# The head of a conditioned decoder layer: column groups of the modulation by output block, five slices, and an instruction order written out

## The chip, the core and the metric

The kernel runs on one core of one Trainium2 chip. A core has five engines that run side by side, each through its own instructions in order: TensorE (PE, matrix products out of SBUF into PSUM), VectorE (DVE), ScalarE (ACT), GpSimd (POOL) and SyncE (SP). SP and POOL also issue the transfers between HBM and SBUF, each on a queue of its own, and 16 DMA engines carry them. The metric is the device time of one execution in microseconds; lower is better.

## The reference, cut to what matters

One layer runs on 256 prompt rows and 8 x 8 sample rows (320 columns in the kernel, where everything is held transposed). Each of the nine sequences (one prompt, eight samples) has a conditioning vector `c`.

```python
mod = silu(c) @ w_ada + b_ada                 # w_ada: 2048 x (6*2048)
sh1, sc1, g1, sh2, sc2, g2 = split(mod, 6)
h = rmsnorm(x, norm1_g) * (1 + sc1) + sh1
p = h @ w_in                                  # q k v og u ga gb and a narrow gate input
o, s_new = gla(q, k, v, loga, s0)             # gated linear attention, 4 heads
merged = sigmoid(ga) * (rmsnorm(o) * silu(og)) + sigmoid(gb) * pool(u)
x = x + g1 * (merged @ w_o)
h2 = rmsnorm(x, norm2_g) * (1 + sc2) + sh2
x = x + g2 * ((silu(gate) * up) @ w_down)     # gate, up = split(h2 @ w_gu)
```

Outputs are the normed x of both groups, the attention states and the pooling buffers. The head, the part that the change is about, is everything up to `h` and the first quarter of `h @ w_in`: the columns of attention head 0, called group 0.

## The kernel before

**Tiles.** The 2048 input features are 16 blocks of 128 (`KT`). `hh[k]` and `hl[k]` are the high and the low part of block k of h, 128 x 320. A weight arrives as fp32 in a `raw` tile; `split` (line 146) makes its high part on ACT (line 151) and its low part on DVE (line 152), 512 columns at a time; `mm3` (line 164) then makes three products, lines 165 to 167. Group 0 has eleven units of 256 output columns (q, k, two of v, u, two each of og, ga, gb).

**Why there are slices.** The section products of w_ada for shift (section 0) and scale (section 1) must be there before a block of h can be made, and w_ada is large: 2 x 16.8 MB for these two sections. So the head runs over slices of the 16 blocks, `SLICES` (line 39): blocks 0-1, 2-3, 4-7 and 8-15. For each slice all units of group 0 are multiplied with the blocks of that slice and added up in SBUF (`evac`, line 349: the first slice writes, on ACT or DVE; the later ones add on DVE, lines 356, 358 and 369). Meanwhile the next slice's blocks are made in the background: the list `bg` (line 493) holds `hada` for section 0, `hada` for section 1, and `h_unit`, for two blocks at a time, and is worked off evenly between the units.

**One `ada` call** (line 214) makes one section for two blocks: four loads of 512 KB on SP's queue into a ring of seven buffers, 16 matmuls with 256 columns of w_ada as moving data, four of them side by side in 32-column strips of the array, each strip summing every fourth input block; then a copy to SBUF (line 228), two transposes, a reduction over the four strips (line 233), and the additions of bias, one and norm weight (lines 236 to 240).

**One `h_unit`** (line 454) takes per block three transposes of the x rows, a copy to `xT` on ACT, which POOL stores to DRAM for later (line 463), the scaling by the row norm (line 462), `affine` (lines 320 to 322) and `hilo` (lines 315 and 316).

**Units.** q, k and u go through `proj` (256 columns, one PSUM tile of the two in pool `pmain`); v, og, ga and gb through `proj2` (line 196: 512 columns, both PSUM tiles at once).

**What sets the order.** A scheduler that simulates the program's timeline picks each engine's order out of the source, with source order as priority; it may pull later work forward. All w_in and w_ada loads of the head are on SP's queue, in an order that it chose. Eight loads of a queue may be under way; a ninth waits for the first. In the second half of the head the narrow gate projection `alr_proj` (line 467) runs, and group 0's first attention steps begin before the last units end.

Behind the head stand the other three heads' projections with attention steps of the head before between them, the sections 4, 2, 3 and 5 of w_ada in bursts (`ada_burst`, line 273), then w_o, w_gu and w_down. None of that is edited.

Of the kernel before, what the change touches and what calls it, by code (L numbers as in the profile page):

```python
# [11 lines left out]
F32 = mybir.dt.float32  # L12
# [8 lines left out]
P = 128  # L21
TP, NB, LS = 256, 8, 8
TS = NB * LS
T = TP + TS
# [14 lines left out]
SLICES = ((0, 2), (2, 4), (4, 8), (8, 16))  # L39
# [43 lines left out]
def body(tc, A):  # L83
# [112 lines left out]
    def proj2(w, col, k0, k1, xh, xl):  # L196

        pp = [pmain.tile([P, 2, 512], F32, tag="pm", name=nm("ps")) for _ in range(2)]
        for c0 in range(k0, k1, 2):
            nk = min(2, k1 - c0)  # L200
            for j, whi, wlo in split_chunk(w[:, c0:c0 + nk, col:col + 512], nk, 512):
                kt = c0 + j
                for i in range(4):
                    mm3(pp[i // 2][:, i % 2, :T], whi[:, i * P:(i + 1) * P], wlo[:, i * P:(i + 1) * P],
                        xh[kt], xl[kt], kt == k0, kt == k1 - 1)
        return pp

# [5 lines left out]

    def ada(sec, b0, nb=2, pool=None, bufs=2):

        pool = pool or apool[0]
        blk = sec * KT + b0
        w = nb * P
        ps = misc()
        step = 8 // nb  # L220
        for k0 in range(0, KT, step):
            raw = raw_chunk(wada[:, k0:k0 + step, blk * P:(blk + nb) * P], step, w, pool, "araw", bufs)
            for i in range(step):
                j, r = (k0 + i) % 4, (k0 + i) // 4
                PE.matmul(ps[32 * j:32 * j + 32, 0:w], lhsT=scT[:, k0 + i, :], rhs=raw[:, i, :],
                          start=r == 0, stop=r == 3, tile_position=(0, 32 * j))
        sb = pool.tile([P, w], F32, tag="adasb", name=nm("adasb"))
        S.copy(sb, ps[:, 0:w])
        pt = misc()
        for i in range(nb):  # L230
            tr(pt[:, i * P:(i + 1) * P], sb[:, i * P:(i + 1) * P])
        dst = mod[:, blk:blk + nb, :]
        V.tensor_reduce(dst, pt[:, 0:w].rearrange("p (b j r) -> p b r j", b=nb, j=4)[:, :, 0:9, :],
                        axis=AX.X, op=ALU.add)
        bb = bada[:, blk:blk + nb].unsqueeze(2).broadcast_to([P, nb, 9])
        V.tensor_tensor(dst, dst, bb, op=ALU.add)
        if sec in (1, 4):
            g = N1G if sec == 1 else N2G
            V.tensor_scalar(dst, dst, 1.0, None, op0=ALU.add)
            V.tensor_tensor(dst, dst, g[:, b0:b0 + nb].unsqueeze(2).broadcast_to([P, nb, 9]), op=ALU.mult)  # L240


# [69 lines left out]
    hl = [hp.tile([P, T], F32R, tag="hl%d" % k, name="hl%d" % k) for k in range(KT)]  # L312
# [5 lines left out]
    def affine(x, a, b, kt):  # L318

        V.tensor_scalar(x[:, 0:TP], x[:, 0:TP], modp(a, kt), modp(b, kt), op0=ALU.mult, op1=ALU.add)  # L320
        V.tensor_tensor(s3(x[:, TP:T]), s3(x[:, TP:T]), mods(a, kt), op=ALU.mult)
        V.tensor_tensor(s3(x[:, TP:T]), s3(x[:, TP:T]), mods(b, kt), op=ALU.add)
# [74 lines left out]
    with tc.tile_pool(name="head", bufs=1) as xp:  # L397
        junk = xp.tile([P, D], F32, name="junk")
        crow = junk[0:9, :]
        nc.sync.dma_start(crow[0:1, :], A["c_prompt"])  # L400
        nc.sync.dma_start(crow[1:9, :], A["c_sample"])
        xn = [xp.tile([P, D], F32, name="xn%d" % i) for i in range(3)]
        G.memset(xn[2][TS:P], 0.0)
        x2d = A["x_prompt"][0]
        V.memset(scT, 0.0)
        make_identity(nc, ident)
        pt = misc()
        for k in range(KT):
            tr(pt[:, 16 * k:16 * k + 9], crow[:, k * P:(k + 1) * P])
# [15 lines left out]
        def hada(sec, b, nb):  # L425
            ada(sec, b, nb, *head_ring)
# [692 lines left out]
```

## Time and profile before

| | us |
|---|---|
| median of 3 runs | 1977.53 (1976.45 to 1977.74) |
| the profiled execution | 1978.01 |
| its span, first to last instruction | 1976.2 |
| first product of group 0 starts | 40.62 |
| last product of the head ends | 254.3 |
| PE busy in the span | 1927.1 |

The profile is of one execution. Per engine it gives the busy time; the windows give the same for stretches of the span, with the clock granted to PE, the mean busy share of the 16 DMA engines and their GB/s. In a group of instructions stand line, engine, operation, the tiles (out<-in), the count, then busy time and mean duration, then the idle time before them and what ended it. PEld is PE's loading of stationary weights. SPq and POOLq are the queues that issue transfers. A fp32 matmul appears as two records, one with the high and low parts (fp32r) as one.

### The profile page before, as it was taken

How to read it: one execution, taken by the hardware profiler on the slowest of the kernel's cores; microseconds unless marked ns; L12 is line 12 of the kernel's file. 1: busy time of each engine (PE TensorE's matmuls, PEld its weight loads, DVE VectorE, ACT ScalarE, POOL GpSimd, SP SyncE). 2: the span in 40 equal slices, each digit the busy share in tenths (PEclk: the TensorE clock that was granted, in tenths of full speed). 3: DMA queues.
4: the chain of work that ended last, by engine and by line, in shares of the span. 5: the costliest groups of instructions: out<-in, count | busy, mean ns of one | idle time of the engine just before them, and what ended most of it. 6: DMA issues, size and time to landing. Idle time of an engine off the chain costs nothing.

```text
span 1976.2 us, 34764 instructions
## 1 busy us (share of the span) xinstructions
PE 1927.1 (98%) x13852; PEld 1812.4 (92%) x13852; DVE 1005.3 (51%) x1905; ACT 822.5 (42%) x1469; POOL 184.7 (9%) x332
## 2 busy tenths in 40 slices
PE   5999999999999999999999999999999999999997
PEld 3778998988899889988989999999999999999997
DVE  2655655656356535665474444444444444444554
ACT  3323553643336433553354333433333434344443
POOL 1002201221121102111130000000000000000000
PEclk9999999999999999999999999999999999999998
DMA  9995558758865787478944554444444444444442
GB/s 323 342 337 184 198 171 282 254 185 307 281 225 165 270 294 260 129 260 319 326 150 159 183 189 142 150 150 144 158 145 151 150 150 150 151 150 148 149 139 97
DMA packets 310044, 400.93 MB, mean 203 GB/s; under 512 B 12865, under 2 KB 273825, under 8 KB 309545
## 3 DMA queue, kind: packets, MB, share of 16 engines
q1 hardware_dynamic: 279754, 291.17, 45.7%
q0 software_dynamic: 30128, 107.55, 14.7%
q8 instruction: 108, 1.77, 0.4%
q14 instruction: 54, 0.44, 0.1%
HBM read 374.23 MB, written 24.67 MB: 202 GB/s over the span
## 4 chain that ended last, share of the span: by engine, by line
PE 82%; DMA 2%; ACT 1%; DVE 1%; issue 0%; POOL 0%; ACTq 0%; DVEq 0%; POOLq 0%
PE ps L167 25%; PE ps L165 25%; PE ps L166 25%; PE pm L284 3%; PE pm L129 1%; DMA araw<-w_ada 1%; PE pm L779 1%; PE pm L758 1%; PE pm L723 1%; DMA raw<-w_o 1%; DMA raw<-w_in 1%; PE pm L712 0%; DVE wlo L152 0%; PE pm L653 0%; ACT whi L151 0%
## 5 line engine op out<-in xcount | busy, mean ns | idle before, releaser
L152 DVE TENSOR_TENSOR wlo<-raw,whi 128x512 fp32r<-128x512 f32 x952 | 655.7, 693 | 784.3 <-ACT whi L151 773.0
L151 ACT CAST whi<-raw 128x512 fp32r<-128x512 f32 x952 | 586.1, 621 | 919.4 <-PE ps L166 830.2
L165 PE MATMUL ps<-hh,whi 128*128 128x320 f32 x1408 | 442.5, 315 | 2.8 <-ACT whi L151 2.1
L167 PE MATMUL ps<-hh,wlo 128*128 128x320 f32 x1408 | 436.8, 313 | 2.0 <-DVE wlo L152 1.9
L166 PE MATMUL ps<-hl,whi 128*128 128x320 f32 x1408 | 437.0, 311 | 0.0
L165 PE MATMUL ps<-h2h,whi 128*128 128x320 f32 x1408 | 434.6, 309 | 0.0
L166 PE MATMUL ps<-h2l,whi 128*128 128x320 f32 x1408 | 434.3, 309 | 0.0
L167 PE MATMUL ps<-h2h,wlo 128*128 128x320 f32 x1408 | 434.2, 309 | 0.0
L165 PEld LDWEIGHTS ps<-hh,whi 128*128 128x128 f32 x1408 | 265.1, 188 | 27.2 <-issue 16.2
L167 PEld LDWEIGHTS ps<-hh,wlo 128*128 128x128 f32 x1408 | 264.2, 188 | 17.6 <-issue 9.1
L166 PEld LDWEIGHTS ps<-hl,whi 128*128 128x128 f32 x1408 | 265.3, 188 | 4.2 <-issue 3.2
L165 PEld LDWEIGHTS ps<-h2h,whi 128*128 128x128 f32 x1408 | 264.5, 188 | 1.2 <-ACT ah L315 1.2
L166 PEld LDWEIGHTS ps<-h2l,whi 128*128 128x128 f32 x1408 | 264.5, 188 | 0.0
L167 PEld LDWEIGHTS ps<-h2h,wlo 128*128 128x128 f32 x1408 | 264.4, 188 | 0.0
L165 PE MATMUL ps<-ah,whi 128*128 128x320 f32 x704 | 217.7, 309 | 0.0
L166 PE MATMUL ps<-al,whi 128*128 128x320 f32 x704 | 216.5, 308 | 0.0
L167 PE MATMUL ps<-ah,wlo 128*128 128x320 f32 x704 | 216.5, 308 | 0.0
L166 PEld LDWEIGHTS ps<-al,whi 128*128 128x128 f32 x704 | 132.0, 187 | 0.0
L165 PEld LDWEIGHTS ps<-ah,whi 128*128 128x128 f32 x704 | 131.9, 187 | 0.0
L167 PEld LDWEIGHTS ps<-ah,wlo 128*128 128x128 f32 x704 | 131.9, 187 | 0.0
L165 PE MATMUL ps<-mh,whi 128*128 128x320 f32 x256 | 80.2, 313 | 3.0 <-ACT whi L151 2.2
L167 PE MATMUL ps<-mh,wlo 128*128 128x320 f32 x256 | 80.0, 312 | 0.0
(284 smaller groups left out, 1557.0 us busy)
## 6 DMA issues: line engine op xcount, KB each, us to landing
raw<-w_gu SPq DMA_DIRECT2D x176, 512.0 KB, 3.4
raw<-w_in SPq DMA_DIRECT2D x173, 512.0 KB, 3.8
araw<-w_ada POOLq DMA_DIRECT2D x64, 1024.0 KB, 7.9
raw<-w_down SPq DMA_DIRECT2D x80, 512.0 KB, 3.4
raw<-w_ada SPq DMA_DIRECT2D x64, 512.0 KB, 6.3
S<-state_gla POOLq DMA_DIRECT2D x16, 1024.0 KB, 8.4
o_gs<-S POOLq DMA_DIRECT2D x16, 1024.0 KB, 6.1
raw<-w_o SPq DMA_DIRECT2D x32, 512.0 KB, 6.9
```

Source lines behind the costliest of these rows:

```text
L129: PE.transpose(out, in_, ident[:k, :k])
L151: S.copy(hi, raw)
L152: V.tensor_sub(lo, raw, hi.bitcast(F32))
L165: PE.matmul(ps, lhsT=whi, rhs=xhi, start=start, stop=False)
L166: PE.matmul(ps, lhsT=whi, rhs=xlo, start=False, stop=False)
L167: last_mm[:] = [PE.matmul(ps, lhsT=wlo, rhs=xhi, start=False, stop=stop).ins]
L284: last_ada[:] = [PE.matmul(ps[32 * j:32 * j + 32, 0:2 * P], lhsT=scT[:, k0 + r, :], rhs=ada_raw[n][:, r, 2 * j * P:(2 * j + 2) * P], start ...
L723: PE.matmul(pt, lhsT=E["kdn"][:, s, d * P:(d + 1) * P], rhs=E["vn"][:, s], start=s == 0, stop=s == 1)
L758: PE.matmul(pt[32 * j:32 * j + 32, :], lhsT=qeP[:, d, 4 * gg + j, :], rhs=E["S0", gg, d][:, j], start=False, stop=d == 0, tile_position=(0 ...
L779: PE.matmul(pt, lhsT=E["kpn"][:, j, d * P:(d + 1) * P], rhs=E["vp"][:, gg], start=True, stop=True)
```

## The change

The diff rewrites the head. What it does:

- `SLICES` becomes 0-1, 2-3, 4-7, 8-11, 12-15.
- **Column groups by output block.** The class `Ada` makes both sections for a slice's blocks together. A `burst` multiplies two or four input blocks; the four strips of the array hold four column groups (the two sections, in halves) instead of four input blocks, and the sum over the input blocks is made in PSUM. There is one copy, one or two transposes, and per section an addition that also brings in the bias (plus one for section 1 as well: it is added to the bias beforehand); no reduction. A two-block slice has four bursts of 16 matmuls with 128 columns, a four-block slice eight bursts of 8 matmuls with 256 columns.
- **Queues.** The w_ada loads of the first slice stay on SP's queue, right behind x; those of the later ones go to POOL's queue, as do the small vectors. The ring has nine buffers.
- **Units.** All units have 256 columns and one PSUM tile. Slices are cut into pieces of two blocks and 256 columns (12 products). Two-block slices load w_in in chunks of 2 blocks x 512 columns, four-block slices in chunks of 4 x 256. The split of a weight (`cut`) stands three pieces ahead of its products (`mul`).
- **x.** The first eight blocks of x are transposed, and scaled by the row norm, ahead of the first product; they are held in two `merged` tiles and stored to DRAM in the last slice. The other eight follow in slices 2 and 3. `x_mod` (affine and hilo) makes h in the last pieces of the slice before.
- **Order.** From the head's start to the last slice all engines take their instructions in source order (`tc.manual_schedule()`); the background work has fixed places (`bg[n]` behind piece n). From the last slice on the scheduler orders as before.
- The constants for the gate projection are loaded in slice 3 rather than at the start; the conditioning vectors are loaded as 128 rows of 128 numbers and transposed by two instructions instead of 16.

The core of the diff:

```diff
-SLICES = ((0, 2), (2, 4), (4, 8), (8, 16))
+SLICES = ((0, 2), (2, 4), (4, 8), (8, 12), (12, 16))
+XE = 8
...
+        manual = ExitStack()
+        manual.enter_context(tc.manual_schedule())
...
-        nc.sync.dma_start(vr0, A["b_ada"].rearrange("o (r p) -> (o r) p", p=P))
+        nc.gpsimd.dma_start(vr0, A["b_ada"].rearrange("o (r p) -> (o r) p", p=P))
...
+        def cut(p):
+            if p < len(pieces):
+                u, k, c, (ks, cs), _, _ = pieces[p]
+                cuts[p] = split(raws[c][:, ks, cs])
+                if p + 1 == len(pieces) or pieces[p + 1][2] != c:
+                    load(c + 4)
...
+        def mul(p):
+            (kind, i, col), k, c, _, first, last = pieces[p]
+            if first:
+                ps_now[0] = pmain.tile([P, 2, 512], F32, tag="pm", name=nm("ps"))
...
+            if last:
+                evac(ps, g0, kind, i, 0 if k < 2 else 1)
...
+            def burst(self):
...
+                for i in range(step):
+                    for j in range(4):
+                        PE.matmul(self.ps[32 * j:32 * j + 32, 0:w // 2], lhsT=scT[:, k0 + i, :],
+                                  rhs=raws[j // 2][:, i, (j % 2) * (w // 2):(j % 2 + 1) * (w // 2)],
+                                  start=k0 + i == 0, stop=k0 + i == KT - 1, tile_position=(0, 32 * j))
...
+            def close(self):
...
+                for q in range(nq):
+                    tr(pt[:, q * P:(q + 1) * P], self.sb[:, q * P:(q + 1) * P])
...
+        adas = [Ada(k0, k1 - k0, nc.sync if k0 == 0 else nc.gpsimd) for k0, k1 in SLICES]
+        for n in range(3):
+            adas[0].load()
+        load(1)
+        adas[0].load()
+        load(3)
...
+        def x_mod(k):
+            x = xp.tile([P, T], F32, tag="xh", bufs=2, name=nm("xh"))
+            affine(x, xqs[k], 1, 0, k)
+            hl[k] = hp.tile([P, T], F32R, tag="hl%d" % k, name="hl%d" % k)
+            hilo(hh[k], hl[k], x)
...
+            last = si == len(SLICES) - 1
+            slots = 11 if k1 - k0 == 2 else 22
+            bg = [[] for _ in range(slots)]
+            if not last:
                 n0, n1 = SLICES[si + 1]
...
+                nxt = adas[si + 1]
+                nb = 4 if n1 - n0 == 2 else 8
+                room = slots - 4
+                for b in range(nb):
+                    bg[0].append(nxt.load)
+                for b in range(nb):
+                    bg[1 + b * (room - 1) // nb].append(nxt.burst)
+                bg[room].append(nxt.out)
+                bg[room].append(nxt.close)
+                for k in range(n0, n1):
+                    if k >= XE:
+                        bg[2 + 3 * (k - n0)].append(lambda k=k: (x_tr(k, S.copy), x_norm(k), x_spill(k)))
+                    bg[room + (k - n0) * 3 // (n1 - n0)].append(lambda k=k: x_mod(k))
+            if si == 3:
+                bg[4].append(late_loads)
+            if si == 4:
+                manual.close()
+                for k in range(XE):
+                    x_spill(k)
+                bg[3].append(lambda: alr_proj(walr, cum))
+            for n in range(slots):
+                p = firsts[si] + n
+                cut(p + 3)
+                mul(p)
+                for f in bg[n]:
+                    f()
```

More of the change, by code (lines that the diff above doesn't have):

```diff
@@ L194, in projs @@
         return pp
[L196 to L206, printed above, removed]
     wada = A["w_ada"][0].rearrange("(kt p) n -> p kt n", p=P)
@@ L212, in body @@
     wdn = A["w_down"][0].rearrange("(kt p) n -> p kt n", p=P)
[L214 to L240, printed above, removed]
     NBA = 8
@@ new lines, in body @@
+        V.memset(scT, 0.0)
+        V.memset(xn[2][TS:P], 0.0)
+        ssq = xp.tile([P, 3, 2], F32, name="ssq")
+        V.memset(ssq, 1.0)
+        us = units(0)
+        walr = xp.tile([P, KT, 16], F32, name="walr")
+        cum = xp.tile([P, NM0 + NM1 + NMS], F32, name="cum")
+        chunks, pieces, firsts = [], [], []
+        for k0, k1 in SLICES:
+            firsts.append(len(pieces))
+            if k1 - k0 == 2:
+                at = 0
+                while at < len(us):
+                    kind, i, col = us[at]
+                    pair = at + 1 < len(us) and us[at + 1][0] == kind
+                    for j in range(2 if pair else 1):
+                        pieces.append((us[at + j], k0, len(chunks), (slice(0, 2), slice(256 * j, 256 * j + 256)), True, True))
+                    chunks.append((col, k0, 2, 512 if pair else 256))
+                    at += 2 if pair else 1
+            else:
+                for u in us:
+                    for j in (0, 2):
+                        pieces.append((u, k0 + j, len(chunks), (slice(j, j + 2), slice(0, 256)), j == 0, j == 2))
+                    chunks.append((u[2], k0, 4, 256))
@@ new lines, in body @@
+        ps_now = [None]
+        def mul(p):
+            (kind, i, col), k, c, _, first, last = pieces[p]
+            if first:
+                ps_now[0] = pmain.tile([P, 2, 512], F32, tag="pm", name=nm("ps"))
+            ps = ps_now[0]
+            hi, lo = cuts.pop(p)
+            for j in range(2):
+                for f in range(2):
+                    mm3(ps[:, f, :T], hi[:, j, f * P:(f + 1) * P], lo[:, j, f * P:(f + 1) * P], hh[k + j], hl[k + j],
+                        first and j == 0, last and j == 1)
+            if last:
+                evac(ps, g0, kind, i, 0 if k < 2 else 1)
@@ new lines, in body @@
+        junk = xp.tile([P, D // 2], F32, name="junk")
+        for i in range(3):
+            n = P if i < 2 else TS
+            for c in range(2):
+                S.activation(junk[:n], xn[i][:n, c * (D // 2):(c + 1) * (D // 2)], AF.Square,
+                             accum_out=ssq[:n, i, c:c + 1])
+        rst = xp.tile([P, 3], F32, name="rst")
+        V.tensor_tensor(rst, ssq[:, :, 0], ssq[:, :, 1], op=ALU.add)
+        S.activation(rst, rst, AF.Sqrt, scale=1.0 / D, bias=epst)
+        V.reciprocal(rst, rst)
@@ L430, in body @@
+        first.burst()
         pt = misc()
```

187 lines of the change are left out of this document (110 added, 77 removed).

## The prediction, made before the change was run

> **What bounds the kernel now.** I read the page first (engine totals, slices), then the table of windows, cut where the head's stages change, then the timeline of the first 41 us, the groups of instructions, and last the waits of SP's queue.
>
> ```profile
> span 1976.2 us, 34764 instructions
> PE 1927.1 (98%) x13852; PEld 1812.4 (92%) x13852; DVE 1005.3 (51%) x1905; ACT 822.5 (42%) x1469; POOL 184.7 (9%) x332
> PE   5999999999999999999999999999999999999997
> DMA  9995558758865787478944554444444444444442
> raw<-w_ada SPq DMA_DIRECT2D x64, 512.0 KB, 6.3
> ```
>
> PE is the bound nearly everywhere; what it does not fill lies in the first slice (49 us), where the DMA digits stand at 9. The change touches only the head, and everything behind it waits for PE, so a microsecond won in the head is one won at the end. The windows divide it:
>
> ```profile
> core 0: us, PE busy (x) PEld busy (x) DVE busy (x) ACT busy (x) POOL busy (x), PEclk, DMA share, GB/s
> 0.00:10.00 10.00, 1.87 (x16) 1.78 (x16) 0.99 (x6) 2.58 (x3) 6.15 (x14) 1.00 0.81 241
> 10.00:20.00 10.00, 1.25 (x10) 0.59 (x10) 0.57 (x4) 6.37 (x8) 0.00 (x0) 1.00 0.90 240
> 20.00:30.00 10.00, 7.47 (x58) 1.63 (x50) 1.55 (x7) 0.97 (x3) 0.00 (x0) 1.00 1.05 359
> 0.00:40.60 40.60, 17.97 (x140) 8.40 (x140) 9.22 (x35) 13.58 (x20) 7.27 (x16) 1.00 0.96 308
> 68.60:99.40 30.80, 30.80 (x254) 23.83 (x254) 20.72 (x51) 9.77 (x22) 2.15 (x4) 1.00 0.98 335
> 162.10:254.30 92.20, 89.69 (x615) 86.72 (x614) 53.29 (x109) 45.30 (x84) 23.59 (x53) 0.98 0.56 182
> 1400.00:1500.00 100.00, 69.93 (x228) 42.54 (x227) 1.00 0.47 153
> ```
>
> The first projection product starts at 40.6, the last of group 0 ends at 254.3: 213.7 us. The last row is one line (L165) of the steady stage. Lines 166 and 167 run as often there, so 684 products take 100 us, 0.146 us each, although the trace shows each as 0.31 long. A "busy" PE can therefore stand still half the time, and I count instructions, not busy time. From 68.6 to 99.4 the 16 DMA engines are full; behind 162 they are at 0.56. The head has an entry that waits for data, a middle where transfers and PE are level, and an end that is pure PE.
>
> **Entry: when does the first product start?**
>
> ```profile
> 12.95 8.57 SPq L143 DMA_DIRECT2D raw<-w_ada  x7
> 32.11 1.08 PE L225 MATMUL pm<-raw,scT 128*32 128x256 f32 x8 [2.27 <-DMA raw<-w_ada]
> 33.32 0.37 ACT L228 COPY adasb<-pm 128x256 f32<-128x256 f32 x1 [1.87 <-PE pm L225]
> 35.16 0.18 DVE L240 TENSOR_TENSOR mod<-mod,vec 128x18 f32<-128x18 f32 x1
> 37.89 0.49 DVE L320 TENSOR_SCALAR xh<-xh,mod 128x256 f32<-128x256 f32 x1
> 39.53 0.82 ACT L315 CAST hh<-xh 128x320 fp32r<-128x320 f32 x2
> 40.62 0.57 PE L165 MATMUL ps<-hh,whi 128*128 128x320 f32 x2
> SPq L143 <- DMA xn<-x_prompt: 6.2, 1, 6.2
> SPq L143 <- PE pm L225: 72.8, 40, 5.5
> ```
>
> The first w_ada load is issued only at 12.95: eleven loads (conditioning, x, vectors) stand ahead of it on SP, and it waits 6.2 us for an x load to land. Until 20 us DMA moves 240 GB/s, then 359. The last w_ada chunk of slice 0 is used at 32.11; 8.5 us pass to the first product, because the scale of x and its transposes come behind it.
>
> The change puts the six small vector loads on POOL's queue and the late constants out of the entry, so w_ada follows x at once. Ahead of the last group of slice 0 lie 0.07 MB conditioning, 2.62 MB x, 4.19 MB w_ada and one 0.52 MB chunk of w_in: 7.4 MB, at 359 GB/s 20.6 us, plus some 2 us in which nothing moves yet: about 23. Behind it remain one burst (1.1), the copy (0.37), one transpose, three small additions (0.18 each), affine, copy and subtraction: by these rows 4.8 us with gaps, since the squares, x transposes and their scaling now lie ahead, in the wait for data. That gives 28.
>
> But slice 1's w_ada goes out on POOL's queue meanwhile. One of nine buffers is free at once, and each early burst frees two more; up to five loads (2.6 MB, 7 us) can share the engines with the group that the first product waits for. Ends: 28 and 36. I take 32, half of them ahead: 8.6 us gained.
>
> **Work of PE from the first product to the head's end.**
>
> ```profile
> L225 PE MATMUL pm<-raw,scT 128*32 128x256 f32 x412 | 33.1, 388 | 0.0
> L129 PE MATMUL pm<-cst,xn 128*128 128x128 f32 x42 | 5.7, 273 | 0.0
> L129 PE MATMUL pm<-cst,adasb 128*128 128x128 f32 x26 | 5.1, 278 | 0.6 <-ACT adasb L228 0.5
> L480 PE MATMUL pm<-hh,wal 128*128 128x320 f32 x16 | 4.7, 308 | 0.0
> 40.05 0.64 PE L225 MATMUL pm<-raw,scT 128*32 128x256 f32 x8
> 289.94 0.44 PE pm L129 x4
> 308.24 0.57 PE pm L653 x16
> 488.26 1.00 PE pm L284 x16
> ```
>
> Common: 16 blocks x 22 columns x 3 = 1056 products x 0.146 = 154.4; the gate projection (32 products, L480 and L481) 4.7; group 0's next steps that run inside, about 2.
>
> Before: 412 w_ada records in groups of eight at 0.64: 33.0. (Each matmul of line 225 appears as two records.) 68 transposes at 0.11 (0.44 for four): 7.5. Sum 201.6; measured 213.7, so 12 us are stalls or switching.
>
> After: a burst of the four-block slices is eight matmuls of 256 columns, 16 records, like the L284 row: 1.00; 24 of these. A two-block burst is 16 matmuls of 128 columns; line 653 has that shape, 16 records in 0.57, so 32 cost 1.14; four of these lie behind the first product. Together 28.6. Transposes: 8 x-blocks x 3, the other eight being done in the entry, and 7 of w_ada sums, 31 x 0.11 = 3.4. With the common 161.1 that is 193.1: 8.5 less than before. Spending one more accumulation slice adds 11 DVE additions and no PE instruction.
>
> **Edits costed at nothing.**
>
> ```profile
> L463 POOL DMA_DIRECT2D xspill<-xT x14 | 7.6, 547 | 126.9 <-ACT xT L461 126.9
> ```
>
> The squares in halves, the x copies and the first eight scalings run while the entry waits for w_ada (PE 17.97 busy of 40.6); without that cover each block would put its three transposes, 0.33, back on PE's path. The stores of the first eight x blocks move to POOL's queue in the last slice, ahead of group 0's state loads: 8 x 0.55 us of issue and 1.3 MB, where DMA stands at 0.56. The late constants queue on POOL behind the last group of w_ada loads, in slice 3; the gate projection needs them 21 pieces later, over 37 us. The 11 more accumulations stand in the DVE count that follows.
>
> **New stalls, from the order written out.**
>
> ```profile
> L152 DVE TENSOR_TENSOR wlo<-raw,whi 128x512 fp32r<-128x512 f32 x88 | 60.0, 698 | 41.7 <-ACT whi L151 41.7
> L369 DVE SCALAR_TENSOR_TENSOR mg<-ps,mg 128x640 f32<-128x640 f32 x11 | 9.0, 821 | 9.3 <-PE ps L167 9.2
> L316 DVE TENSOR_TENSOR hl<-xh,hh 128x320 fp32r<-128x320 f32 x15 | 7.1, 492 | 1.4 <-ACT hh L315 1.2
> L315 ACT CAST hh<-xh 128x320 fp32r<-128x320 f32 x14 | 6.1, 457 | 12.3 <-DVE xh L322 12.3
> L320 DVE TENSOR_SCALAR xh<-xh,mod 128x256 f32<-128x256 f32 x14 | 5.7, 407 | 0.1
> L321 DVE TENSOR_TENSOR xh<-xh,mod 128x64 f32<-128x64 f32 x14 | 3.0, 218 | 0.0
> ```
>
> A piece of 12 products takes PE 1.75 us; DVE needs 0.70 for its split and 0.82 for an accumulation, each piece in a two-block slice, each second piece in a four-block one. So DVE keeps up in general. The x_mod of one block occupies DVE for 1.7 us: 0.41 + 2 x 0.22 small, then it stands still while ACT copies (0.46), then 0.49. Behind it on DVE are queued the next split and the next accumulation, and PE waits for that accumulation, with two PSUM tiles.
>
> Slice 1 puts four x_mods into pieces 7, 7, 8 and 9. Counting from the end of piece 7: accumulation 0.8, group close 0.6, two x_mods 3.4, split 0.7, accumulation of piece 8 done at 6.2; piece 10 would start at 3.8 and starts at 6.2; piece 11 loses 1.5 more: 4 us. In four-block slices an accumulation comes every 3.5 us and the same count leaves 2 us each, in slices 2 and 3. Slice 0: 2 us, where six x_norms stand ahead of a split. The tail is scheduled as before, and I keep 2 us of its stalls. Sum 12, no less than before, with ends 4 and 20.
>
> Transfers, as a check: until slice 1's last burst 2.6 + 16.8 + 5.3 = 24.7 MB must land, at 335 GB/s 74 us after the first 2. PE gets there at 32 + 26 + some 19 = 77. They are level; a shortfall is in the upper end.
>
> **Sum.** 32 + 193 + 12 = 237 against 254.3: 17 us less. The profiled execution took 1978.0 (span 1976.2 and 1.8 around it), 0.5 above the median of 1977.5; 1978.0 - 17 = 1961.0, on the median's scale 1960.5. A difference below 0.2% (4 us) can hardly be told from none.
>
> **Rivals.**
> Both gains in full (0.20): start at 28 and 4 us of stalls, 28 + 197 = 225, 29 us less: 1949. For it speaks that the list of waits has SP held 72.8 us by PE's use of w_ada, with w_in loads queued behind; two queues end that. Against it stands the DMA share of 0.98.
>
> POOL's loads crowd the entry (0.14): start 36 to 40 and the middle paced by transfers: 38 + 193 + 15 = 246, 8 us less: 1969.
>
> POOL's loads come late (0.06). If they reach half of 335 GB/s, slices 1 to 4 (29.4 MB, begun at about 14) are in at 190, where PE would use the last at 182; PE stands at the burst, in order: 8 us of the 17 go, 1969. In the trace POOL issued the 14 stores of the row above beside a DVE that was busy for two thirds of a window, with no stretch to be seen.
>
> [...]
>
> The gain is given back behind the head (0.06): the automatic order resumes in a slice half as long, so group 0's gate chain starts later and PE waits where it did not; no change within 4 us, 1977.
>
> In-order DVE loses (0.09), the other side. Fifty-five units end in an accumulation that the second next unit waits for. If each loses 0.7 us on DVE, 38 us go where 17 were won: 1998. It decides at 0.3 us a unit. Against it: 0.70 + 0.82 is less than 1.75, and the splits run three pieces ahead.
>
> **How the numbers follow.** The forecast itself has 0.45. Its own range comes from the ends of start (28 to 36) and stalls (4 to 20): 1949 to 1973. The rivals on the same side end inside it; left out are the slower case and the outer edges, 0.2 together. So 1948 to 1974. Faster: 0.45 + 0.20 + 0.14 + 0.06 = 0.85; within 0.2%: 0.06; slower: 0.09.
>
> **What would show it.** First product at 32 (28 to 36), with the x transposes ahead of the last w_ada burst; POOL's first w_ada load before 10 us; slice ends near 58, 90, 141 and 191, last product near 237; bursts at 1.0 us; DVE, not DMA, as releaser of PE in pieces 10 and 11 of slice 1; behind the head each step earlier by the same 17. A start past 40, PE waiting for w_ada at bursts, or splits held behind accumulations in every unit would make it wrong.

## The result and the profile after

The changed kernel takes 1993.4 us (median of 4, 1992.4 to 1996.75) against 1977.6 for the kernel before on the same chip (4 runs): ratio 1.0081, 95% interval 1.0069 to 1.0094. It is slower by 0.8%, where 17 us less were forecast. The profiled execution took 1996.75, the slowest of the four, 3.4 above their median. One execution of e15 below (3799 us) and one of the kernel before beside it (3152 us) ran far slower than all others, and no ratio uses them.

The page of the changed kernel: span, engine totals, and PE and DMA in 40 slices.

```profile
span 1995.0 us, 34891 instructions
PE 1922.4 (96%) x13942; PEld 1817.4 (91%) x13942; DVE 1019.5 (51%) x1893; ACT 813.5 (41%) x1456; POOL 227.6 (11%) x393
PE   4999989999999999999999999999999999999997
DMA  9887548747874787469954554444444444444442
```

PE has 4.7 us less busy time in a span 18.8 us longer, so what was lost is standing still, not work. The DMA digits of the first 150 us fell from 999 to 988: the transfers are spread, not denser. The windows of the changed kernel, cut at its first product and at the first product of each slice, show where:

```profile
core 0: us, PE busy (x) PEld busy (x) DVE busy (x) ACT busy (x) POOL busy (x), PEclk, DMA share, GB/s
0.00:42.50 42.50, 12.90 (x164) 9.53 (x164) 9.39 (x32) 12.78 (x23) 15.68 (x32) 0.90 0.99 317
42.50:71.90 29.40, 27.78 (x262) 25.01 (x262) 17.49 (x39) 12.72 (x24) 5.63 (x8) 0.91 0.79 279
71.90:107.70 35.80, 30.41 (x263) 23.45 (x263) 20.04 (x41) 8.09 (x15) 11.24 (x16) 1.00 0.92 322
107.70:158.10 50.40, 49.92 (x406) 43.45 (x407) 28.76 (x54) 15.58 (x29) 13.48 (x20) 1.00 0.86 291
158.10:209.90 51.80, 50.77 (x406) 43.55 (x407) 30.98 (x60) 16.52 (x31) 9.88 (x15) 1.00 0.66 215
209.90:260.50 50.60, 46.04 (x300) 44.01 (x301) 34.03 (x69) 22.79 (x46) 17.74 (x41) 1.00 0.61 203
```

The entry grew from 40.6 to 42.5 us, with the DMA engines full (0.99): they moved more than the first product needed. The timeline of PE, of SP's queue and of GpSimd in the changed kernel's entry:

```profile
32.52 0.41 PE L466 MATMUL pm<-araw,scT 128*32 128x128 f32 x4 [3.22 <-DMA araw<-w_ada]
37.84 1.92 PE L466 MATMUL pm<-araw,scT 128*32 128x128 f32 x28 [4.90 <-DMA araw<-w_ada]
42.50 0.63 PE L166 MATMUL ps<-hh,whi 128*128 128x320 f32 x1 [1.90 <-ACT hh L274]
3.21 15.65 SPq L450 DMA_DIRECT2D araw<-w_ada  x6
20.26 2.64 SPq L450 DMA_DIRECT2D araw<-w_ada  x2
5.39 0.81 POOL L450 DMA_DIRECT2D araw<-w_ada  x1
22.36 1.50 POOL L450 DMA_DIRECT2D araw<-w_ada  x2 [16.16 <-PE pm L466]
24.37 2.25 POOL L536 DMA_DIRECT2D xspill<-mg  x4 [0.51 <-DVE mg L533]
26.61 1.51 POOL L450 DMA_DIRECT2D araw<-w_ada  x2
```

The last two loads of slice 0 are issued from 20.26 on. GpSimd issues four loads and four x stores between 22.36 and 28.1, and four more stores behind them, and PE has the last of the two only at 37.84. At 310 GB/s, the mean of the first 37.84 us, 11.7 MB move until then; 7.4 MB were needed. From there the chain takes 4.7 us, as forecast (4.8).

**How the loss stands to the forecast.** The profiled execution is 35.8 us above the forecast's 1961.0. The first product starts 10.5 us later than forecast (42.5 for 32). From there to the start of the head's last product go 217.9 us (260.4 less 42.5) for a forecast of 205, 12.9 more. From there to the span's end go 1734.6 for the 1721.9 of before (1976.2 less 254.3), 12.7 more. (The 254.3 in the table of before is the start of that product; it ends at 254.6.) These three make 36.1; the forecast's sum came to 17.3 and was rounded to 17, which is the 0.3 between. Of the last 12.7, up to 3.4 can belong to this one execution, which lies that much above the median.

### The profile page after: what moved, and what is told of

It is laid out like the page before. It is cut to its first block, busy times and chain, and to the rows that moved or that the text cites. A ratio compares the mean times of both kernels' runs of the same rounds, so it can differ in the third digit from the quotient of the medians.

```text
span 1995.0 us, 34891 instructions
## 1 busy us (share of the span) xinstructions
PE 1922.4 (96%) x13942; PEld 1817.4 (91%) x13942; DVE 1019.5 (51%) x1893; ACT 813.5 (41%) x1456; POOL 227.6 (11%) x393
## 4 chain that ended last, share of the span: by engine, by line
PE 71%; DMA 2%; DVE 1%; ACT 0%; issue 0%; POOL 0%; ACTq 0%; DVEq 0%; POOLq 0%
PE ps L166 22%; PE ps L168 22%; PE ps L167 22%; PE pm L243 2%; DMA raw<-w_o 2%; PE pm L130 1%; DMA araw<-w_ada 0%; PE pm L878 0%; PE pm L899 0%; PE pm L843 0%; DVE wlo L153 0%; DVE acc L918 0%; PE pm L832 0%; DVE x L1082 0%; PE pm L773 0%
## 5 line engine op out<-in xcount | busy, mean ns | idle before, releaser
L219 POOL DMA_DIRECT2D araw<-w_ada x64 | 45.8, 718 | 339.7 <-PE pm L243 330.7
```

The source lines that it names most:

```text
L219: nc.gpsimd.dma_start(t[:, r:r + 2], wada[:, k0 + r:k0 + r + 2, col:col + NBA * P])
```

## The experiments

"Gate step" in the table is the first product of group 0's gates with `alr` (line 562 before, 682 after), which needs the gate projection; "to it" is how far it stands behind the end of the head's last product, and "rest" the time from that end to the span's end. The end is taken with the last product's duration, 0.3 us later than its start. "264th" is the first product behind 264 others, that is the first one of slice 2 (two slices of two blocks, 22 columns, three products each); in the same way the 528th is the first behind eight blocks and the 792nd the first behind twelve. All from the profiled executions; the medians are from all runs.

| kernel | median | ratio, 95% | first product | 264th | head end | to it | rest |
|---|---|---|---|---|---|---|---|
| before | 1977.6 | | 40.6 | 100.2 | 254.6 | -19 | 1721.6 |
| after | 1993.4 | 1.0069-1.0094 | 42.5 | 107.7 | 260.7 | +17 | 1734.3 |
| e1 | 1999.6 | 1.0096-1.0126 | 34.4 | 111.1 | 265.3 | +17 | 1733.6 |
| e2 | 1997.2 | 1.0080-1.0114 | 45.0 | 107.3 | 261.8 | +16 | 1733.9 |
| e3 | 1997.7 | 1.0089-1.0119 | 32.1 | 108.5 | 263.7 | +16 | 1730.4 |
| e4 | 2003.9 | 1.0118-1.0148 | 49.4 | 116.7 | 268.8 | +16 | 1734.8 |
| e6 | 1986.1 | 1.0028-1.0058 | 40.2 | 99.8 | 256.4 | +10 | 1727.4 |
| e7 | 1977.9 | 0.9993-1.0012 | 43.8 | 103.3 | 252.9 | -20 | 1725.9 |
| e9 | 1999.3 | 1.0095-1.0125 | 42.2 | 102.9 | 262.2 | +16 | 1733.7 |
| e10 | 1988.5 | 1.0037-1.0069 | 44.0 | 107.1 | 260.6 | 0 | 1725.3 |
| e11 | 1985.5 | 1.0032-1.0057 | 40.2 | 99.8 | 256.7 | +14 | 1729.9 |
| e12 | 1974.9 | 0.9982-1.0000 | 36.8 | 96.3 | 251.8 | -20 | 1726.7 |
| e13 | 1995.0 | 1.0073-1.0101 | 42.4 | 102.5 | 259.1 | +17 | 1734.5 |
| e14 | 1986.0 | 1.0030-1.0055 | 42.4 | 104.5 | 259.4 | 0 | 1724.7 |
| e15 | 1981.7 | 1.0010-1.0034 | 31.0 | 93.2 | 248.0 | +16 | 1731.3 |
| e16 | 1967.7 | 0.9937-0.9964 | 38.8 | 98.3 | 245.6 | -42 | 1722.5 |
| e17 | 1978.8 | 0.9997-1.0015 | 38.7 | 98.4 | 255.9 | -42 | 1721.7 |
| e18 | 1978.9 | 1.0000-1.0018 | 39.9 | 95.3 | 252.0 | -18 | 1722.7 |
| e19 | 1972.3 | 0.9958-0.9981 | 36.4 | 95.5 | 246.9 | -19 | 1722.7 |
| e20 | 1990.0 | 1.0043-1.0074 | 43.9 | 105.6 | 257.2 | +15 | 1737.0 |

### The entry: who crowds whom (e1, e2, e3)

```diff
e1 (changed kernel):
-        adas = [Ada(k0, k1 - k0, nc.sync if k0 == 0 else nc.gpsimd) for k0, k1 in SLICES]
+        adas = [Ada(k0, k1 - k0, nc.sync if k0 <= 2 else nc.gpsimd) for k0, k1 in SLICES]
e2 (changed kernel; e3 is e1 and e2 together):
                 bg[4].append(late_loads)
+                for k in range(XE):
+                    bg[6 + k].append(lambda k=k: x_spill(k))
             if si == 4:
                 manual.close()
-                for k in range(XE):
-                    x_spill(k)
```

> The changed kernel with slice 1's w_ada loads on SP's queue instead of POOL's, behind the loads of slice 0. Crowding theory: in the changed kernel five POOL loads of w_ada (2.6 MB) and eight stores of x (1.3 MB) share the engines with the last two loads of slice 0 between 22 and 38 us; without the five, at about 350 GB/s, those land 6 to 7 us earlier, the first product starts at 35 to 36 instead of 42.5, and the kernel takes about 1986. Rival, late issue: the seventh and eighth w_ada load are issued only at 20.3 and 21.5 because a queue has eight loads under way, and they take their 12 to 16 us whatever else moves; first product at 41 to 43, time within 2 of 1993. A third: the start moves, but SP's queue now holds w_in back in slice 0 and the gain is lost there; slice 0 longer than its 29 us.

> The changed kernel with the stores of the first eight x blocks written into the hand order, behind pieces 6 to 13 of slice 3, instead of behind its end, from where they were pulled forward to 24 us. Crowding theory: 1.3 MB less beside the last loads of slice 0, about 3.7 us; first product near 39, kernel near 1989. Late issue: first product stays at 41 to 43 and the time within 2 of 1993.

> Both edits at once: slice 1's w_ada on SP, the first eight x stores in slice 3. Crowding theory: the two add up, first product at 31 to 32, as much as I had forecast, PE does not fall to the half clock before it (2 us more), kernel near 1981. Late issue: 41 to 43 and 1993. If the start is at 31 and the kernel is still above 1978, the rest of the loss lies in the slices and behind the head.

With slice 1's loads behind slice 0's on SP, the start comes at 34.4; with the x stores out of the way as well at 32.1, the forecast's number. The stores alone give nothing (45.0). But the time does not follow, it grows to 1999.6 and 1997.7: slice 0 then lasts 42 to 43 us in place of 29, because its bursts for slice 1 wait (8.6 us in e3, and PE's granted clock is 0.80 in that slice, 0.91 in the changed kernel). e3's timeline of PE:

```profile
32.07 0.42 PE L166 MATMUL ps<-hh,whi 128*128 128x320 f32 x1 [2.08 <-ACT hh L274]
44.62 0.64 PE L466 MATMUL pm<-araw,scT 128*32 128x128 f32 x4 [6.00 <-DMA araw<-w_ada]
```

So the crowding sets the start, and an early start is worth nothing where it is paid for with late loads: PE takes the burst in its order and stands in front of it. (e15 below has an early start without late loads, and keeps it.)

### The order written out (e4)

```diff
-        manual.enter_context(tc.manual_schedule())
```

> The changed kernel without the hand order: the same instructions, queues and places, but the scheduler orders all engines in the head too. Order theory: what source order costs is the excess of 24 us beside the products (13 before) and the group 0 steps that are no longer pulled forward under the last slices (8 us behind the head); without it the stretch from the first to the last product of the head falls from 218 to about 206 and the kernel takes about 1975 even if the start stays at 42. Rival: the column groups and the queue are the loss and the order is not; then the time stays within 4 of 1993. A third: the scheduler sends the w_ada loads of all slices off early and the start comes later than 45; slower than 1993.

Without it the changed kernel is 10 us slower yet and starts at 49.4, as the third of its expectations had it. Taking the written order away wins nothing back, so it is not what loses against the kernel before; what the scheduler would make of another source is not shown.

### Slices, and the place of the gate projection (e6, e11, e17, e10)

```diff
e6 (kernel before):
-SLICES = ((0, 2), (2, 4), (4, 8), (8, 16))
+SLICES = ((0, 2), (2, 4), (4, 8), (8, 12), (12, 16))
e11 (kernel before; e17 has ui == 0):
-                if si == len(SLICES) - 1 and ui == 1:
+                if si == len(SLICES) - 1 and ui == 4:
e10 (changed kernel; both groups of w_ada for blocks 8 to 15 in slice 2, w_in of the last slice in chunks of four blocks):
-SLICES = ((0, 2), (2, 4), (4, 8), (8, 12), (12, 16))
+SLICES = ((0, 2), (2, 4), (4, 8), (8, 16))
...
-            if si == 4:
+            if si == 3:
                 manual.close()
```

> The kernel before, with its order, its queue and its bursts, but with the slices 2-2-4-4-4 of the change. The gate projection of group 0 needs all 16 blocks; in the trace before it stands at 180 us, in the changed kernel at 225, and the attention steps behind the head come 26 us later there. Cover theory (the gate chain has less of the head left to hide in): the projection moves to about 220, the last product of group 0 ends near 257, the distance to the span's end grows by 8 us or more, 1985 to 1992. Rival (the loss behind the head comes from the order written out or from the new bursts, not from the slices): 1977 within 4, the first attention products within 5 us of 277.

> The kernel before with one number changed: the gate projection is put behind the fifth group of units of the last slice in place of the second, so that it runs near 212 us, where the five-slice version of the kernel before had it (214), and not at 180. Slices, bursts, order and queue stay. Cover theory (the place of the gate projection sets what is lost behind the head): head end 253 to 257, first transposed values of group 0 near 281 in place of 273, 1983 to 1987. Rival (the extra accumulation slice does it, the projection has slack): 1977.5 within 2.

> The kernel before with the gate projection behind the first group of units of the last slice, not the second: some 7 to 14 us earlier. 35 us later cost 7.6. If that cost is in proportion (0.2 us for each us): 1975 to 1976. If the chain has slack at its place in the kernel before, which I think likelier, as the gate step that follows it stands at 235, 19 us before the head's end: 1977.5 within 2.

> The changed kernel with the slices 2-2-4-8 of before: slices 3 and 4 are one slice of eight blocks, both groups of w_ada for blocks 8 to 15 go through slice 2, the x_mods of these blocks end there, the automatic order resumes at the start of the eight-block slice, and the gate projection stands in its fourth piece. Cover theory: gate projection near 175, head end 245 to 252 (slice 2 paced by transfers, one accumulation slice less), distance from there to the end as before, 1721 to 1724; 1966 to 1977. Rival (order written out costs behind the head, whatever the slices): distance 1730 or more, 1978 to 1990.

The five slices alone cost the kernel before 8.7 us (1986.1 to 1977.4), and only 1.8 of them stand at the head's end. The late gate projection alone, in the old slices, costs 7.6 (1985.5 to 1977.95 on its chip), and 2.1 of it at the head's end. So not the extra accumulation loses the time but what moves with it. The gate projection needs all 16 blocks of h; they are complete when the last slice starts, and a last slice half as long leaves the chain behind it half the cover, that is half the products that can run while it takes its time. The rows of its first product, of the gate step and of the first attention step, in the kernel before, the changed one and e11:

```profile
180.10 0.31 PE L480 MATMUL pm<-hh,wal 128*128 128x320 f32 x1
235.22 0.51 PE L562 MATMUL pm<-w,alr 128*128 128x256 f32 x3
272.84 1.09 PE L129 MATMUL pm<-cst,vTP 128*128 128x128 f32 x8
```

```profile
224.43 0.31 PE L601 MATMUL pm<-hh,wal 128*128 128x320 f32 x1
277.35 0.62 PE L682 MATMUL pm<-w,alr 128*128 128x256 f32 x3
283.22 0.39 PE L166 MATMUL ps<-hh,whi 128*128 128x320 f32 x1 [2.66 <-DVE mg L1005]
297.58 1.09 PE L130 MATMUL pm<-cst,vTP 128*128 128x128 f32 x8
490.99 0.41 PE L166 MATMUL ps<-hh,whi 128*128 128x320 f32 x1 [2.12 <-DVE mg L1005]
```

```profile
215.92 0.31 PE L480 MATMUL pm<-hh,wal 128*128 128x320 f32 x1
270.67 0.52 PE L562 MATMUL pm<-w,alr 128*128 128x256 f32 x3
278.86 1.10 PE L587 MATMUL pm<-cumr,w 128*128 128x272 f32 x4 [2.19 <-ACT w L575]
287.96 1.09 PE L129 MATMUL pm<-cst,vTP 128*128 128x128 f32 x8
```

From projection to gate step 53 to 55 us pass in these three: the gate step stands 19 us ahead of the head's end before, 14 to 17 behind it in the others. But the distance is no fixed length. It is 52 us in e6, 44.5 in e17, 34 in e16, and 72 in e10, whose gate projection comes only 9 us later than before:

```profile
188.66 0.31 PE L603 MATMUL pm<-hh,wal 128*128 128x320 f32 x1
260.47 0.52 PE L688 MATMUL pm<-w,alr 128*128 128x256 f32 x3
```

`alr` is made 6 to 7 us behind the projection (187.21 before, 230.08 after). The gate step also reads a tile that DVE makes from a small weight, which GpSimd loads: loaded from 215.34 and made at 228.02 before, 249.96 and 267.29 in e11, 260.81 and 276.82 in the changed kernel, whose gate step starts as the tile is done. In e10 it is there at 233.85, 27 us ahead. So a late projection makes the gate step late (e11), and something else can as well (e10); what holds it up in e10 stays open.

The attention steps come 15 to 25 us later, the scheduler pulls other products forward in their stead, and PE then waits where it did not (2.66 and 2.12 us in the changed kernel, 2.19 in e11). The last two columns of the table are this cost against the place of the gate step: from -42 to -18 the rest is 1722 (e7 and e12 excepted), at 0 it is 1725, at +10 1727, at +14 1730, at +15 to +17 1730 to 1737. Some profiled executions lie well above their medians (e12 by 5.3 us, e7 by 2.7, the changed kernel by 3.4, e11 by 2.8, e20 by 6.0). With what each lies above or below its median taken off, the order is the same: 1720 to 1725, then 1725 to 1726, 1728 and 1727, and 1731 to 1735.

In the changed kernel PE is busy for 1704.3 of the rest's 1734.3 us, in the kernel before for 1699.2 of 1721.6, in e11 for 1703.1 of 1729.9: it stands idle 7.5 and 4.4 us longer than before. In the changed kernel its clock also falls to half for 3.41 us at 283.54 and again at 491.75, where the kernel before keeps the full clock; 15 instructions run in each of these stretches, and at 0.147 us a product some 23 would, so the two cost about 2.4 us by this estimate. e17 shows that the chain has slack in the kernel before: earlier gains nothing (0.9997 to 1.0015).

e10 goes the other way: the old slices in the changed kernel bring the gate step from +17 to 0, the rest to 1725.3, and win 5 us. That is less than the 1966 to 1977 expected: they do not bring the head's end forward (260.6). Slice 2, which now carries w_ada for eight blocks, takes 62.4 us in place of 50.4 (63.3 in the kernel before), and from its start to the head's end 153.5 us pass, in the changed kernel 153.0.

### DVE's part (e9, e13, e14, e20)

```diff
e9 (changed kernel):
-                    bg[room + (k - n0) * 3 // (n1 - n0)].append(lambda k=k: x_mod(k))
+                    bg[room + (k - n0)].append(lambda k=k: x_mod(k))
e13 (changed kernel):
+                    bg[room + (k - n0) * (4 if slots == 11 else 3) // (n1 - n0)].append(lambda k=k: x_mod(k))
e14: e10 and e13 together
e20 (changed kernel; sums over slices of q, k, v and gates left out):
-            if acc:
-                V.scalar_tensor_tensor(dst, src, sc, dst, op0=ALU.mult, op1=ALU.add)
-            elif i == 0:
+            if acc or i == 0:
                 S.activation(dst, src, AF.Copy, scale=sc)
```

> The changed kernel, with one x_mod in each of the last four pieces of a four-block slice, in place of 2-1-1 in three. The trace shows PE waiting for DVE's accumulations 2.97 and 1.57 us there in slice 1. If DVE is what slice 1 loses by: those waits shrink below 1.5 together, 264th product 3 us earlier (104), time 1988 to 1991. If transfers pace slice 1 whatever DVE does: 264th at 107 within 1.5, time within 3 of 1993.

> The changed kernel with the x_mods of blocks 4 to 7 one to a piece in the last four pieces of slice 1, and the later slices as in the changed kernel. Spreading them in all slices had the 264th product at 102.9 in place of 107.7, and lost it again in slice 3, where the last x_mod stood behind the last piece. If that reading is right: 264th near 103, 528th near 154, 792nd near 206, 1988 to 1990. Rival (the 4.8 us are given back by the transfers of slices 2 and 3 whatever is done with x_mods): 792nd at 209 or more, 1992 to 1996.

> The changed kernel with the slices 2-2-4-8 and the x_mods of blocks 4 to 7 spread over four pieces: the two repairs together. If the costs add up: 264th at 103, head end 256, 1983 to 1985. Rival (slice 2 is paced by its transfers, all 8.4 MB of w_ada for eight blocks and 5.8 MB of w_in, so an earlier start of it buys nothing): 528th at 169 or more, 1988 within 3.

> The changed kernel with the sums over slices of q, k, v and the gates left out: where DVE added a slice's result to the earlier ones, ACT copies it, so every value of these units holds the last slice alone. The trace of the changed kernel has 12 us of waits of products for DVE (sums 7.6, splits 3.2, subtractions 1.1) and 2.6 for ACT. If DVE's sums make them: under 5 us in all, head end 250 to 254 (260.4), 1984 to 1988. If PE's stalls sit elsewhere, or the waits move to ACT: head end 258 or later, 1991 to 1996.

PE's waits at the end of slice 1 in the changed kernel, and the queue on DVE ahead of the first of them:

```profile
101.04 0.41 DVE L279 TENSOR_SCALAR xh<-xq,mod 128x256 f32<-128x256 f32 x1
102.36 0.49 DVE L275 TENSOR_TENSOR hl<-xh,hh 128x320 fp32r<-128x320 f32 x1 [0.52 <-ACT hh L274]
102.89 0.69 DVE L153 TENSOR_TENSOR wlo<-raw,whi 128x512 fp32r<-128x512 f32 x1
103.49 0.82 DVE L328 SCALAR_TENSOR_TENSOR mg<-ps,mg 128x640 f32<-128x640 f32 x1
104.37 0.42 PE L166 MATMUL ps<-hh,whi 128*128 128x320 f32 x1 [2.66 <-DVE mg L328]
107.66 0.39 PE L166 MATMUL ps<-hh,whi 128*128 128x320 f32 x1 [1.26 <-DVE mg L328]
```

Two x_mods, a split and then the accumulation that PE waits for, as the prediction counted it. With the x_mods spread, e13 reaches the 264th product 5.2 us earlier (102.5). Most of it is given back: 1.5 us are left at the first product of slice 3 (156.6 to 158.1), 1.6 at the head's end, and the median is no better. e9, with the x_mods of all slices spread, lost the gain between the 528th and the 792nd product (54.8 us, 51.8 in e13 and in the changed kernel). e14 adds old slices and spread x_mods and has 1986.0, 7 us better than the change; of the 2.6 us that it won on e10 in slice 1, 0.7 were left at the end of slice 2 (168.82 to 169.56). e20 lies between its two expectations: the head from first to last product is 213.3 in place of 218.2, the waits for DVE fall from 12.0 to 4.6, but those for ACT rise from 2.6 to 7.1, and the median gains 3.4.

### Transfers (e7, e15, e16)

```diff
e7 (kernel before):
-        last_raw[:] = [nc.sync.dma_start(t, src).ins]
+        last_raw[:] = [(nc.gpsimd if tag == "araw" else nc.sync).dma_start(t, src).ins]
e15 (changed kernel; e16 the same in the kernel before: half of each w_ada load left out, the other half used twice):
-                    self.q.dma_start(raw, wada[:, k0:k0 + step, c0:c0 + w])
+                    self.q.dma_start(raw, wada[:, k0:k0 + step // 2, c0:c0 + w])
...
-                                  rhs=raws[j // 2][:, i, (j % 2) * (w // 2):(j % 2 + 1) * (w // 2)],
+                                  rhs=raws[j // 2][:, i // 2, (j % 2) * (w // 2):(j % 2 + 1) * (w // 2)],
```

> The kernel before with one edit: the head's w_ada loads go out on GpSimd's queue. Transfer theory (until the 264th product the head is paced by what the DMA engines move): 264th product at 100 within 4 as before, time 1977 within 5. Queue theory A (SP was held 72.8 us by PE's use of w_ada and w_in stood behind it): 264th product at 90 to 95, 1965 to 1972. Queue theory B (a second queue crowds the entry and costs as in the changed kernel): first product past 44, 264th past 104, 1982 or more.

> The changed kernel, with half of the bytes of each of the head's w_ada loads left out (every row block that is loaded is used twice, so the modulation is another one); as many loads, bursts, buffers and instructions as before. If transfers pace the head: first product at 34 or less, 264th near 92 (107.7), head end near 242 (260.5), 1975 to 1981, the late gate projection still costing its 8. If stalls of the written order pace it: the start moves by 5 or more, the 264th less than 6, 1988 or more.

> The kernel before, with half of the bytes of each of the head's w_ada loads left out in the same way. If its slices 0 to 2 are paced by transfers (DMA share 0.93 to 1.03): 528th product near 148 (163.5), head end 243 to 248 (255.6), 1964 to 1970. If PE or the order of the work paces them: 528th at 158 or more, 1973 or more.

GpSimd's queue for w_ada is no loss in itself: e7 starts 3.2 us later, makes it good by the 528th product, and has the time of the kernel before. Half the bytes tell where transfers count. The windows of e15, cut as above:

```profile
0.00:31.00 31.00, 11.57 (x163) 8.94 (x163) 9.21 (x31) 12.78 (x23) 13.57 (x30) 1.00 0.93 280
31.00:60.10 29.10, 27.15 (x262) 24.04 (x262) 17.50 (x39) 12.83 (x24) 5.96 (x11) 0.94 0.68 222
60.10:93.20 33.10, 30.35 (x262) 24.14 (x263) 20.01 (x41) 8.09 (x15) 8.51 (x16) 0.96 0.68 223
93.20:144.00 50.80, 50.30 (x407) 43.85 (x407) 28.85 (x54) 15.69 (x29) 10.68 (x20) 0.99 0.66 210
144.00:195.80 51.80, 50.76 (x407) 43.54 (x407) 31.06 (x60) 16.54 (x31) 8.64 (x15) 1.00 0.57 174
195.80:247.80 52.00, 47.55 (x300) 45.51 (x301) 35.52 (x71) 22.77 (x46) 17.77 (x41) 0.97 0.62 199
```

The start falls to 31.0, and behind it nothing is won: the head from first to last product takes 217.0 in place of 218.2, with the DMA engines at 0.57 to 0.68. Given its start, the changed head is paced by PE and its own waits. But the 11.5 us of the start are kept to the end: the median is 11.7 lower (1981.7). e16 is the other way round: its start moves by 1.8 us, its head shrinks from 214.0 to 206.8, and the median is 10 us lower; the 528th product comes at 154.6, between its two expectations. The kernel before was paced by transfers for a part of its head: with light ones, PE's 201.6 us of counted work leave 5 us of stalls.

### What pays by itself (e12, e18, e19)

```diff
e12 (kernel before; the norm vectors in the same way):
-        nc.sync.dma_start(vr0, A["b_ada"].rearrange("o (r p) -> (o r) p", p=P))
+        nc.gpsimd.dma_start(vr0, A["b_ada"].rearrange("o (r p) -> (o r) p", p=P))
e18: e12, and w_ada of slices 1 and on by nc.gpsimd
e19: e12, and in the automatic order for each two blocks
-                    bg += [lambda b=b, nb=nb: hada(0, b, nb), lambda b=b, nb=nb: hada(1, b, nb),
+                    bg += [lambda b=b: hada2(b),
with hada2 making both sections in one PSUM tile by column groups, as the change does
```

> The kernel before with its six small vector loads moved from SP's queue to GpSimd's, and nothing else: the one part of the change that frees the entry without adding traffic to it. If the late issue of w_ada (first at 12.95 us, 240 GB/s until 20 us) paces slices 0 to 2: first product 37 to 39, 528th 3 to 5 us earlier (159), 1972 to 1975. Rival (x and its chain set the first product, and the ring of buffers the rest): first product 40, 1977 within 2.

> The kernel before with the vector loads on GpSimd's queue and the w_ada loads of slices 1 and on behind them on the same queue; slice 0's stay on SP. Moving the vectors alone gave 1974.9, all w_ada on GpSimd 1977.9 with a start at 43.8 and slices 1 and 2 six us shorter. If slice 1's loads crowd the entry as in the changed kernel: first product 41 or later, 1975 to 1979. If they queue behind the vectors late enough: first product 37 to 39, 528th near 152, 1970 to 1974.

> The kernel before, in its own slices and automatic order, with two parts of the change: the vector loads on GpSimd's queue (alone: 1974.9) and the sums of w_ada by output block in one PSUM tile for both sections (one copy and one transpose for two blocks, in place of two and four). The bursts cost PE the same 4.1 to 4.5 us for two blocks; the transposes saved are 24 x 0.11 = 2.6 us. If PE's work counts in the head once the entry is repaired: head end near 250 (252.8), 1972 to 1974. If transfers hide it, or a sum that needs both sections comes later than two of one each: 1975 to 1979.

The vectors on GpSimd's queue alone bring the start to 36.8 and 3.0 us; the interval, 0.9982 to 1.0000, ends at no change. With the second queue on top the gain is gone (e18, 1.0000 to 1.0018); neither of its expectations held in full: the start came at 39.9, the 264th product early (95.3), and the head's end no earlier than in e12. With the column groups as well, e19 takes 1972.3, 0.3% faster than the kernel before (0.9958 to 0.9981) and 1% faster than the change. Its windows, the entry in two and then to the 264th, the 528th and the last product:

```profile
0.00:20.00 20.00, 3.62 (x37) 2.88 (x41) 0.98 (x6) 7.27 (x7) 9.22 (x20) 1.00 0.91 281
20.00:36.40 16.40, 11.05 (x167) 8.28 (x159) 6.79 (x24) 5.61 (x12) 1.13 (x2) 1.00 1.08 386
36.40:95.50 59.10, 58.61 (x644) 51.31 (x644) 33.66 (x73) 22.48 (x43) 2.16 (x5) 1.00 0.97 340
95.50:153.40 57.90, 57.90 (x724) 52.86 (x723) 35.20 (x84) 20.00 (x40) 4.27 (x8) 1.00 1.03 356
153.40:247.80 94.40, 91.44 (x654) 88.67 (x651) 52.54 (x107) 45.67 (x87) 23.98 (x53) 0.98 0.59 184
```

281 GB/s in the first 20 us (before 241), then the DMA engines full until the 528th product, which comes ten us earlier than before, and the gate step still 19 us ahead of the head's end. Of the ten, 7.7 are left at the head's end and 6.0 in the median.

## Why the prediction was wrong, step by step

Three steps failed: the start (10.5 us), the stalls (12.1) and the distance behind the head (12.7). The work of PE was right.

- **The first product at 32, half of slice 1's loads ahead: failed.** It came at 42.5. Five of GpSimd's loads stood ahead, the whole of the upper end, and the x stores, put in the last slice, went out at 24 to 35 us; the last two loads of slice 0 waited at SP until 20.26. The rival "POOL's loads crowd the entry" had this mechanism, with 36 to 40; the 42.5 lies beyond its end, and its middle paced by transfers was not seen (e15). e3 starts at 32.1, but with no load of slice 1 in the way, where the working had 28: it is the forecast's number and not its sum. The sum had 359 GB/s from 2 us on; the first 32 us of e3 moved 262, the first 20 of the changed kernel 261. What a start is worth was right: in e15 the 11.5 us are kept. In e3 they are lost, because the loads that were pushed back are needed 12 us later.
- **Work of PE, 193.1: right.** 217.9 us less 24.1 of standing between products is 193.8. Bursts took 30.4 for 28.6, of which 1.5 is one wait for w_ada, transposes 2.7 for 3.4.
- **New stalls 12, "no less than before": failed, 24.1.** Counted as what lies beyond 0.15 us from one product's start to the next instruction, the kernel before has 13.3 us, of which 7.7 are ended by no engine (nearly all where PE changes from products to bursts or transposes and back), 1.5 are products at half clock, and 2.2 are ended by DVE and 1.9 by ACT. The changed kernel has 12.0 by DVE and 2.6 by ACT, close to the 12 that were counted, but on top of 7.1 of the first kind and 2.4 at half clock. The working took the new stalls in place of the old ones. Of their place, slice 1's 4 us were right (2.66 and 1.26, e13).
- **Transfers level with PE at slice 1: right as a sum, wrong in use.** They pace the start (e15), and they paced a part of the head of the kernel before (e16). Inside the changed head little hangs on them (217.0 us for 218.2 in e15). By the same count the work there fell from 200.4 us (213.7 less 13.3) to 193.8, and standing rose from 13.3 to 24.1: 6.6 less and 10.8 more make the head 4.2 us longer.
- **"Behind the head each step earlier by the same 17": failed, 12.7 later.** The rival "the gain is given back behind the head" had the mechanism, at 0.06 and priced to end at no change. The step that failed is that the distance from the head's end to the span's end was taken as fixed. The rival was priced by what was won; it should have been priced by the shift of the gate projection, which the trace of before shows at 180 with 55 us to the gate step, 19 ahead of the head's end. Behind the head e6 has 5.8 and e11 8.3 us more than the kernel before by their traces (7.0 and 5.5 by their medians, of 9.7 for the changed kernel). Idle time and half clock account for some 10 of the 12.7. Why the changed kernel loses more there than e6 stays open; e3 and e15, with the same slices, have 9 to 10.
- **In-order DVE as the loser (0.09, 1998): the time came near, the mechanism not.** No loss in every unit: 0.7 us a unit would be 38 us; DVE's waits are 12, in 15 places. And e4 shows the written order ahead of the automatic one.
- **"POOL's loads come late" (0.06): not seen.** Behind the first product PE waits once for w_ada, 1.47 us in slice 1 (94.95), and slices 2 to 4 show no such wait. In e7 all of the head's w_ada goes out on that queue, in the time of the kernel before.

## What to carry to other kernels

Before a stage is cut shorter or finer, follow what starts when the stage has all of its input: put 36 us later, as in e11, its chain ended behind the work that had covered it, and 7.6 us came back as waits behind the edit; put earlier, as in e17, it gained nothing. Price a saving by the resource that paces that stretch, which an experiment with half the bytes tells within one run. And take a large change apart: here two small parts of it are worth 0.3% (e19), while the slices alone cost 0.4% (e6), and with the old slices the changed kernel is still 0.5% slower (e10).

## What the runs showed of the hardware

The clock granted to PE falls to half at or behind some of its waits. In the changed kernel it does so at 34.36, after 3.22 and within 4.90 us of waiting, and is full again only at 48.02, 13.66 us later:

```profile
28.00:34.36 6.36, 1.71 (x26) 1.05 (x18) 1.99 (x4) 0.41 (x1) 1.74 (x4) 1.00 1.04 377
34.36:48.02 13.66, 7.92 (x48) 6.65 (x49) 6.17 (x19) 3.95 (x8) 3.52 (x6) 0.50 0.95 334
48.02:60.00 11.98, 11.98 (x167) 10.61 (x169) 5.48 (x11) 4.46 (x8) 4.22 (x6) 1.00 0.85 295
```

It falls for 3.41 us at 283.54, behind a wait of 2.66 us, and again at 491.75, behind one of 2.12; in the kernel before it falls for 3.41 us at 245.74, after a wait of 1.29 and within one of 0.82 us. But behind the wait of 2.66 us ahead of 104.37 in the changed kernel it stays full. What tells these waits apart, the traces do not show. The half clock takes 2.4 us of the changed kernel's head behind the first product and, by the estimate above, about 2.4 us in the two falls behind the head.

One DVE subtraction took 3.17 us where the same form took 0.83 elsewhere, beside a multiplication on GpSimd, and PE waited 0.62 us for the split behind it. DVE's and GpSimd's rows in the changed kernel:

```profile
257.80 3.17 DVE L275 TENSOR_TENSOR dl<-w,dh 128x640 fp32r<-128x640 f32 x1
258.68 1.59 POOL L346 TENSOR_TENSOR og<-og,sg 128x640 f32<-128x640 f32 x1
```

The subtraction ends 0.70 us behind the multiplication (260.97 and 260.27), about its own usual time. The kernel before has such a pair too: a split that takes 0.69 elsewhere took 1.64 us from 244.28, beside a multiplication from 243.82 to 245.37. Not every DVE instruction beside one is longer: in the changed kernel an accumulation from 251.93 took its usual 0.82 us, beside a multiplication from 251.94 to 253.50. For the subtraction the overlap is 1.59 us and the excess 2.34; ahead of the multiplication GpSimd was issuing stores (until 258.66), and whether these held the subtraction for the other 0.75 is not shown, nor is why the two DVE instructions took longer.
